# Feed-forward gate and up as seven half products per pair of blocks

## The chip, the cores and the metric

The kernel runs on one core of a Trainium2 chip. The metric is device time in microseconds of one launch. Before the change it is 1845.98 us, the median of three runs from 1844.38 to 1849.32. The engines named here are TensorE (PE, with its weight loads shown as PEld), VectorE (DVE), ScalarE (ACT), GpSimd (POOL) and the DMA queues, of which SP issues nearly all.

## The reference, cut to what matters

The kernel computes a whole two-part network for 512 rows of width 1024 in float32: a feed-forward layer, two attention branches that are merged, a second feed-forward layer, a chunkwise recurrent mixer and a gated linear recurrence, with norms and residuals between. Only the two feed-forward layers are touched:

```
def rms_norm(x, g):
    y = x * rsqrt(mean(x * x, axis=-1) + EPS)
    return y * g

def swiglu(x, w_gate, w_up, w_down):
    return (silu(x @ w_gate) * (x @ w_up)) @ w_down

h = h + 0.5 * swiglu(rms_norm(h, ffn1_norm), ffn1_w_gate, ffn1_w_up, ffn1_w_down)
...
h = h + 0.5 * swiglu(rms_norm(h, ffn2_norm), ffn2_w_gate, ffn2_w_up, ffn2_w_down)
```

The weights are 1024 by 2816 for gate and up and 2816 by 1024 for down.

## The kernel before, in words

Activations lie transposed: the 1024 features are 8 tiles of 128 partitions, each 512 columns (the rows of x) wide. These are `h[0..7]`. A float32 product is made as three fp32r products: every operand is split in a high part (a cast on ACT) and a low part (a subtraction on DVE), and `mm3` (L111) issues high by high, high by low and low by high into one PSUM bank.

`wload` (L92) brings 128 by 1024 weights (512 KB) by one DMA on SP into a `raw` buffer (3 of them), and splits them into `hi` and `lo` (5 buffers each; ACT L97, DVE L99). It is given a higher priority, so that the scheduler puts it ahead of other work. The order of the instructions on each engine is fixed when the program is built, by a scheduler that follows the order of the code and these priorities; an engine then runs its list in order.

`ffn` (L203) works in 22 blocks of 128 features of gate and up. `operand` (L132) makes the split operand from `h` times the norm's gain, without the row factor 1/rms; that factor is a column factor here, kept in `rb`, and is multiplied in when a bank is read out (L196, L216). So the first four groups (`pre`) can run before `stats` (L189) has made `rb`: sums of squares on PE (L170), a power on POOL (L178), a transpose on PE (L184), a copy on DVE (L186). A `group` (L143) is 8 blocks of the contraction by 3 matmuls of 512 columns, 24 matmuls. Each block takes one group for gate and one for up; then come tanh on ACT (L198), two products on DVE (L200, L217) and the split (L121, L123). After 8, 8 and 6 blocks the eight output tiles of down get their share (`wload(dn...)`, a group, and L223 adds it to `h`).

Pools that matter: `ap` has 40 buffers of 128 by 512 for activations, `xp` 18 more (`chain`), `pp` and `qp` 4 PSUM banks each (`bank`, `cbank`), `vp` 5 (`v`).

## Time and profile before

| what | before |
|---|---|
| median of three runs | 1845.98 us |
| the profiled execution, its own time | 1849.27 us |
| its span, first to last instruction | 1847.2 us |
| PE busy | 1822.0 us, 99% |
| DVE busy | 1083.3 us, 59% |
| ACT busy | 709.8 us, 38% |
| POOL busy | 23.9 us, 1% |
| mean granted TensorE clock | 0.996 |
| DMA moved | 169.53 MB, 92 GB/s |

The page counts matmuls as busy from issue to the modelled end, and they overlap; so PE's 99% says only that PE had nearly always something to do. How fast the work goes is read from the distance between the starts of neighbouring matmuls. The first feed-forward layer takes about 371 us of the span, the second about 364 us.

### The profile page before, as it was taken

The numbers are of one execution on the slowest core, as the hardware profiler recorded it, in microseconds if no ns is written. First come the engines' busy times: TensorE is split into PE (matmuls) and PEld (weight loads), VectorE is DVE, ScalarE is ACT, GpSimd is POOL, SyncE is SP. The second block draws the span as 40 slices with busy tenths as digits, with TensorE's granted clock in tenths as the row PEclk, the third lists the DMA queues.
The fourth block names the chain that finished last, engine by engine and source line by source line (L and its number), as shares of the span: only waits on it lengthen the run. The fifth ranks groups of instructions, "written<-read, shape, count | busy, mean of one in ns | idle before, by whom it ended". The sixth has DMA issues, their size and how long they took to land.

```text
span 1847.2 us, 21163 instructions
## 1 busy us (share of the span) xinstructions
PE 1822.0 (99%) x8320; PEld 1478.5 (80%) x8320; DVE 1083.3 (59%) x1728; ACT 709.8 (38%) x1050; POOL 23.9 (1%) x53
## 2 busy tenths in 40 slices
PE   8999999999999999999999999999999999999998
PEld 6888888877776688788888888788887888888886
DVE  5544535644646465543543566867467466788785
ACT  4322312424344533222222253533434344446762
POOL 0000000000000000000000000000000000000000
PEclk9999999999999999999999999999999999999999
DMA  5323232333322123232333232222232232232222
GB/s 185 103 92 102 92 103 83 100 101 102 112 69 69 46 91 103 80 103 92 99 95 103 71 122 81 80 80 92 69 102 86 74 103 69 90 97 90 89 69 80
DMA packets 50018, 169.53 MB, mean 92 GB/s; under 512 B 5760, under 2 KB 5888, under 8 KB 49920
## 3 DMA queue, kind: packets, MB, share of 16 engines
q1 hardware_dynamic: 48048, 164.91, 27.5%
q10 hardware_dynamic: 1872, 3.29, 0.5%
q8 instruction: 65, 1.06, 0.2%
q14 instruction: 33, 0.27, 0.0%
HBM read 164.77 MB, written 2.10 MB: 90 GB/s over the span
## 4 chain that ended last, share of the span: by engine, by line
PE 83%; issue 13%; DVE 2%; ACT 1%; POOL 1%; DMA 0%; SPq 0%; POOLq 0%; ACTq 0%; DVEq 0%
PE bank L112 25%; PE bank L114 25%; PE bank L113 25%; PE cbank L679 1%; PE cbank L447 1%; PE cbank L112 1%; PE cbank L113 1%; PE cbank L114 1%; PE cbank L415 1%; POOL small L178 1%; PE cbank L702 1%; PE cbank L703 1%; PE cbank L704 1%; PE cbank L384 0%; ACT hi L97 0%
## 5 line engine op out<-in xcount | busy, mean ns | idle before, releaser
L112 PE MATMUL bank<-act,hi 128*128 128x512 f32 x1944 | 761.2, 393 | 6.6 <-ACT act L138 6.5
L113 PE MATMUL bank<-act,hi 128*128 128x512 f32 x1944 | 761.1, 392 | 1.1 <-DVE act L123 0.5
L114 PE MATMUL bank<-act,lo 128*128 128x512 f32 x1944 | 760.1, 391 | 0.0
L97 ACT CAST hi<-raw 128x1024 fp32r<-128x1024 f32 (+2 forms) x315 | 323.2, 1027 | 829.5 <-PE bank L113 546.5
L99 DVE TENSOR_TENSOR lo<-raw,hi 128x1024 fp32r<-128x1024 f32 (+2 forms) x315 | 375.2, 1192 | 137.9 <-ACT hi L97 137.4
L112 PEld LDWEIGHTS bank<-act,hi 128*128 128x128 f32 x1944 | 366.3, 189 | 87.6 <-ACT act L138 6.5
L113 PEld LDWEIGHTS bank<-act,hi 128*128 128x128 f32 x1944 | 366.4, 188 | 81.7 <-DVE act L123 3.7
L114 PEld LDWEIGHTS bank<-act,lo 128*128 128x128 f32 x1944 | 366.6, 189 | 77.2 <-issue 1.9
L196 DVE TENSOR_TENSOR act<-bank,rb 128x512 f32<-128x512 f32 x70 | 48.3, 690 | 117.8 <-PE bank L114 117.7
L223 DVE SCALAR_TENSOR_TENSOR h<-bank,h 128x512 f32<-128x512 f32 x48 | 33.2, 692 | 112.2 <-PE bank L114 111.7
L216 DVE TENSOR_TENSOR act<-bank,rb 128x512 f32<-128x512 f32 x42 | 29.0, 691 | 101.1 <-PE bank L114 101.1
L112 PE MATMUL bank<-hi,act 128*128 128x512 f32 x224 | 87.8, 392 | 0.0
L114 PE MATMUL bank<-hi,act 128*128 128x512 f32 x224 | 87.3, 391 | 0.0
L113 PE MATMUL bank<-lo,act 128*128 128x512 f32 x224 | 87.2, 389 | 0.0
L121 ACT CAST act<-act 128x512 fp32r<-128x512 f32 x96 | 59.6, 621 | 69.2 <-DVE act L217 28.7
L123 DVE TENSOR_TENSOR act<-act 128x512 fp32r<-128x512 f32 x96 | 65.9, 686 | 12.9 <-ACT act L121 12.4
L802 DVE SCALAR_TENSOR_TENSOR act<-act,vec 128x511 f32<-128x511 f32 (+2 forms) x84 | 62.7, 746 | 1.7
L112 PE MATMUL bank<-chain,hi 128*128 128x512 f32 x160 | 62.7, 393 | 0.0
L114 PE MATMUL bank<-chain,lo 128*128 128x512 f32 x160 | 62.5, 391 | 0.0
L113 PE MATMUL bank<-chain,hi 128*128 128x512 f32 x160 | 62.3, 389 | 0.0
L198 ACT ACTIVATE act<-act 128x512 f32<-128x512 f32 x72 | 45.3, 629 | 30.8 <-DVE act L196 30.5
L200 DVE SCALAR_TENSOR_TENSOR act<-act 128x512 f32<-128x512 f32 x72 | 49.3, 685 | 8.7 <-ACT act L198 8.7
(231 smaller groups left out, 1577.8 us busy)
## 6 DMA issues: line engine op xcount, KB each, us to landing
raw<-in_gu_dram SPq DMA_DIRECT2D x88, 512.0 KB, 3.2
raw<-in_mh_dram SPq DMA_DIRECT2D x64, 512.0 KB, 3.2
raw<-in_win_dram SPq DMA_DIRECT2D x34, 512.0 KB, 3.2
raw<-in_dn_dram SPq DMA_DIRECT2D x32, 512.0 KB, 3.5
raw<-in_mo_dram SPq DMA_DIRECT2D x16, 512.0 KB, 3.2
raw<-in_dn_dram SPq DMA_DIRECT2D x16, 384.0 KB, 3.1
raw<-in_rxr_dram SPq DMA_DIRECT2D x12, 512.0 KB, 3.2
raw<-in_rg_dram SPq DMA_DIRECT2D x12, 512.0 KB, 3.3
```

The source lines that it names most:

```text
L97: S.copy(hi[:, :cols], raw[:, :cols])
L99: V.tensor_tensor(lo[:, :cols], raw[:, :cols], f(hi[:, :cols]), op=ALU.subtract)
L112: PE.matmul(ps, st[0], mv[0], start=start, stop=False)
L113: PE.matmul(ps, st[0], mv[1], start=False, stop=False)
L114: PE.matmul(ps, st[1], mv[0], start=False, stop=stop)
L121: S.copy(hi, x)
L123: V.tensor_tensor(lo, x, f(hi), op=ALU.subtract)
L196: V.tensor_tensor(g, ps, rb, op=ALU.mult)
L198: S.activation(th, g, AF.Tanh, scale=0.5)
L200: V.scalar_tensor_tensor(s, th, 1.0, g, op0=ALU.add, op1=ALU.mult)
L223: V.scalar_tensor_tensor(x[o], ps, 0.25, x[o], op0=ALU.mult, op1=ALU.add)
L802: V.scalar_tensor_tensor(c[:, s:], t[:, : T - s], vc(w, j * nt + i), c[:, s:], op0=ALU.mult, op1=ALU.add)
```

## The change

In both feed-forward layers the first four blocks stay as they were (`plain`). The other 18 are each done as a 2 by 2 product of halves: gate and up are the two rows of the weight side, the lower and upper half of the contraction (4 tiles of 128 each) its columns; the activations are cut in 256 left and 256 right columns. Strassen's scheme (in Winograd's form) makes this product with seven half products instead of eight, from four sums of weight halves (`s1` to `s4`) and four sums of activation halves (`t1` to `t4`). Each half product is 4 by 3 matmuls of 256 columns, so a block takes 84 matmuls of 256 columns in place of 48 of 512.

The activations are normalised first now (`xhalves`, with `rb`), and cut, summed and split once per layer. The weight sums are made per block: one by a DMA that adds onto what lies in SBUF (`G.dma_start` with `accum_op`, issued from POOL), the others by two additions on DVE (`sums`). Seven products go into three PSUM banks and come out through DVE additions. Down is done in chunks of 4 blocks: two output tiles beside each block (`between`), and the last six blocks at the end. `ap` has 34 buffers in place of 40, `raw` 4 in place of 3, and a new pool `gp` two buffers of 128 by 1024 (`four`), which other stages use too.

```diff
--- before.py
+++ after.py
@@ -46,9 +46,10 @@
-    ap = ctx.enter_context(tc.tile_pool(name="ap", bufs=40))
+    ap = ctx.enter_context(tc.tile_pool(name="ap", bufs=34))
     wp = ctx.enter_context(tc.tile_pool(name="wp", bufs=5))
     sp = ctx.enter_context(tc.tile_pool(name="sp", bufs=32))
+    gp = ctx.enter_context(tc.tile_pool(name="gp", bufs=2))
     hp = ctx.enter_context(tc.tile_pool(name="hp", bufs=KD))
     rp = ctx.enter_context(tc.tile_pool(name="rp", bufs=2))
     xp = ctx.enter_context(tc.tile_pool(name="xp", bufs=18))
@@ -91,7 +92,7 @@
     def wload(src, cols=WU):
         with tc.high_priority(offset=BOOST):
-            raw = wp.tile([P, WU], F32, tag="raw", name="raw", bufs=3)
+            raw = wp.tile([P, WU], F32, tag="raw", name="raw", bufs=4)
             nc.sync.dma_start(raw[:, :cols], src)
             hi = wp.tile([P, WU], F32R, tag="hi", name="hi")
             S.copy(hi[:, :cols], raw[:, :cols])
@@ -200,27 +201,207 @@
         V.scalar_tensor_tensor(s, th, 1.0, g, op0=ALU.add, op1=ALU.mult)
         return s
+    def raw_load(parts, adds):
+        raw = wp.tile([P, WU], F32, tag="raw", name="raw", bufs=4)
+        c = 0
+        for src in parts:
+            n = src.shape[-1]
+            nc.sync.dma_start(raw[:, c : c + n], src)
+            c += n
+        if adds is not None:
+            G.dma_start(raw.rearrange("p (r c) -> p r c", r=2), adds.unsqueeze(1).to_broadcast([P, 2, T]),
+                        accum_op=ALU.add)
+        return raw
+    def wsplit(raw):
+        hi = wp.tile([P, WU], F32R, tag="hi", name="hi")
+        S.copy(hi, raw)
+        lo = wp.tile([P, WU], F32R, tag="lo", name="lo")
+        V.tensor_tensor(lo, raw, f(hi), op=ALU.subtract)
+        return hi, lo
+    class Pair:
+        def __init__(self, top, low):
+            self.top, self.low, self.w = top, low, {}
+        def load(self):
+            top, low = self.top, self.low
+            with tc.high_priority(offset=BOOST):
+                self.r2 = raw_load([low[:, T:], top[:, :T]], low[:, :T])
+                self.r1 = raw_load([top], None)
+        def halves(self, raw, one, two):
+            hl = wsplit(raw)
+            self.w[one], self.w[two] = cut(hl, slice(0, T)), cut(hl, slice(T, WU))
+        def first(self):
+            with tc.high_priority(offset=BOOST):
+                self.halves(self.r1, "a11", "a12")
+                self.halves(self.r2, "s1", "s3")
+        def sums(self):
+            r1, r2 = self.r1, self.r2
+            with tc.high_priority(offset=BOOST):
+                V.tensor_tensor(r2[:, :T], r2[:, :T], r1[:, :T], op=ALU.add)
+                V.tensor_tensor(r2[:, T:], r2[:, :T], r1[:, T:], op=ALU.add)
+                self.halves(r2, "s2", "s4")
+        def last(self):
+            with tc.high_priority(offset=BOOST):
+                t = vp.tile([P, T + 32], F32, tag="v", name="v")
+                nc.sync.dma_start(t[:, :T], self.low[:, T:])
+                hi = vp.tile([P, T + 32], F32R, tag="v", name="v")
+                S.copy(hi[:, :T], t[:, :T])
+                lo = vp.tile([P, T + 32], F32R, tag="v", name="v")
+                V.tensor_tensor(lo[:, :T], t[:, :T], f(hi[:, :T]), op=ALU.subtract)
+            self.w["a22"] = cut((hi, lo), slice(0, T))
+    HT = T // 2
+    L, R = slice(0, HT), slice(HT, T)
+    def xhalves(x, gain, rb):
+        b = {n: [] for n in ("b11", "b21", "b22", "t1", "t2", "t3", "t4")}
+        def step(k):
+            xn = []
+            for i in (k, k + 4):
+                t = act_tile()
+                V.scalar_tensor_tensor(t, x[i], gain[:, i : i + 1], rb, op0=ALU.mult, op1=ALU.mult)
+                xn.append(t)
+            one, two = xn
+            b1 = act_tile(F32R)
+            S.copy(b1[:, L], one[:, L])
+            V.tensor_tensor(b1[:, R], one[:, L], f(b1[:, L]), op=ALU.subtract)
+            b["b11"].append((b1[:, L], b1[:, R]))
+            b2 = split(two)
+            b["b21"].append(cut(b2, L))
+            b["b22"].append(cut(b2, R))
+            t12, t34 = ctile(), ctile()
+            V.tensor_tensor(t12[:, L], one[:, L], one[:, R], op=ALU.subtract)
+            V.scalar_tensor_tensor(t12[:, R], t12[:, L], -1.0, two[:, R], op0=ALU.mult, op1=ALU.subtract)
+            V.tensor_tensor(t34[:, L], two[:, R], one[:, R], op=ALU.subtract)
+            V.scalar_tensor_tensor(t34[:, R], t12[:, R], -1.0, two[:, L], op0=ALU.mult, op1=ALU.subtract)
+            for t, n in ((t12, ("t1", "t2")), (t34, ("t3", "t4"))):
+                pr = split(t, ctile)
+                b[n[0]].append(cut(pr, L))
+                b[n[1]].append(cut(pr, R))
+        return b, step
+    def product(ps, w, xk):
+        for k in range(4):
+            mm3(ps, cut(w, slice(k * P, k * P + P)), xk[k], k == 0, k == 3)
+    def quarters(t):
+        return t.rearrange("p (r c) -> p r c", c=HT)
+    def twice(t):
+        return t.unsqueeze(1).to_broadcast([P, 2, HT])
+    def pair_products(pair, b, nxt, between):
+        w = pair.w
+        if nxt:
+            nxt.load()
+        m = bank()
+        product(m[:, L], w["a11"], b["b11"])
+        p1 = ctile()
+        with tc.high_priority(offset=EVAC):
+            S.copy(p1[:, L], m[:, L])
+        c1, c2 = cbank(), cbank()
+        product(c1[:, L], w["a12"], b["b21"])
+        if nxt:
+            nxt.first()
+        between(0)
+        product(c2[:, L], w["s1"], b["t1"])
+        product(c2[:, R], w["s3"], b["t3"])
+        product(c1[:, R], w["s2"], b["t2"])
+        t = gp.tile([P, 2 * T], F32, tag="four", name="four")
+        v = act_tile()
+        with tc.high_priority(offset=EVAC):
+            V.tensor_tensor(quarters(t)[:, 0:4:3], quarters(c1), twice(p1[:, L]), op=ALU.add)
+            V.tensor_tensor(quarters(v), quarters(c2), twice(t[:, 3 * HT :]), op=ALU.add)
+            V.scalar_tensor_tensor(t[:, 3 * HT :], c2[:, R], 1.0, v[:, L], op0=ALU.mult, op1=ALU.add)
+        between(1)
+        c3 = bank()
+        product(c3[:, L], w["s4"], b["b22"])
+        if nxt:
+            nxt.sums()
+        product(c3[:, R], w["a22"], b["t4"])
+        if nxt:
+            nxt.last()
+        with tc.high_priority(offset=EVAC):
+            V.tensor_tensor(t[:, HT : 3 * HT], c3, v, op=ALU.add)
+        g, u = t[:, :T], t[:, T:]
+        th = act_tile()
+        S.activation(th, g, AF.Tanh, scale=0.5)
+        V.scalar_tensor_tensor(g, th, 1.0, g, op0=ALU.add, op1=ALU.mult)
+        V.scalar_tensor_tensor(u, u, -1.0, g, op0=ALU.mult, op1=ALU.mult)
+        return split(u)
     def ffn(x, gain, gu, dn, pre=None):
         xs = operand(x, gain)
         pre = pre or [wload(gu[0])]
         pre = [group(pre[n] if n < len(pre) else wload(gu[n]), xs, (bank if n < 2 else cbank)()) for n in range(4)]
         _, rb = stats(x)
-        for k0 in range(0, KF, 8):
-            k1 = min(KF, k0 + 8)
-            pr = []
-            for j in range(k0, k1):
-                pg, pu = pre[2 * j : 2 * j + 2] if j < 2 else [group(wload(gu[2 * j + i]), xs) for i in range(2)]
-                s = silu2(pg, rb)
-                u = act_tile()
-                with tc.high_priority(offset=EVAC):
-                    V.tensor_tensor(u, pu, rb, op=ALU.mult)
-                V.tensor_tensor(u, u, s, op=ALU.mult)
-                pr.append(split(u))
-            for o in range(KD):
-                w = wload(dn[o][:, k0 * P : k1 * P], (k1 - k0) * P)
-                ps = group(w, pr)
-                with tc.high_priority(offset=EVAC):
-                    V.scalar_tensor_tensor(x[o], ps, 0.25, x[o], op0=ALU.mult, op1=ALU.add)
+        def plain(j):
+            pg, pu = pre[2 * j : 2 * j + 2] if j < 2 else [group(wload(gu[2 * j + i]), xs) for i in range(2)]
+            s = silu2(pg, rb)
+            u = act_tile()
+            with tc.high_priority(offset=EVAC):
+                V.tensor_tensor(u, pu, rb, op=ALU.mult)
+            V.tensor_tensor(u, u, s, op=ALU.mult)
+            return split(u)
+        def down(o, w, base, us):
+            ps = group(w, us, base=base)
+            with tc.high_priority(offset=EVAC):
+                V.scalar_tensor_tensor(x[o], ps, 0.25, x[o], op0=ALU.mult, op1=ALU.add)
+        def down_two(o, k0):
+            c = slice(k0 * P, k0 * P + T)
+            with tc.high_priority(offset=BOOST):
+                raw = raw_load([dn[o][:, c], dn[o + 1][:, c]], None)
+                return wsplit(raw)
+        b, step = xhalves(x, gain, rb)
+        pr = [plain(0), plain(1)]
+        for k in range(4):
+            step(k)
+        pr += [plain(2), plain(3)]
+        def down_job(j):
+            if j >= 20:
+                return lambda i: None
+            o, got, us = 2 * (j % 4), [], old
+            def step(i):
+                if i < 0:
+                    got.append(down_two(o, 4 * (j // 4 - 1)))
+                else:
+                    down(o + i, got[0], 4 * i, us)
+            return step
+        cur = Pair(gu[8], gu[9])
+        cur.load()
+        cur.first()
+        cur.sums()
+        cur.last()
+        old, new = pr, []
+        for j in range(4, KF):
+            nxt = Pair(gu[2 * j + 2], gu[2 * j + 3]) if j + 1 < KF else None
+            job = down_job(j)
+            job(-1)
+            new.append(pair_products(cur, b, nxt, job))
+            cur = nxt
+            if j % 4 == 3 and j < 19:
+                old, new = new, []
+        for o in range(KD):
+            dw = wload(dn[o][:, 16 * P :], 6 * P)
+            down(o, dw, 0, new)
     ffn(h, vc("g1", 0, 8), a["gu1"], a["dn1"], first)
@@ -262,8 +443,9 @@
         rope_t = {}
         def rope_tables():
+            both = gp.tile([P, 2 * T], F32, tag="four", name="four")
             for i in range(2):
-                t = act_tile()
+                t = both[:, i * T : (i + 1) * T]
                 S.dma_start(t, a["rope"][i])
                 rope_t[i] = t
@@ -299,9 +481,16 @@
             S.copy(vb, pv)
             bv.append(vb)
+        room = []
         def gate(i):
             ps = group(wload(win[i]), xs)
-            g = act_tile()
+            if i < 20:
+                if not room:
+                    room.append(gp.tile([P, 2 * T], F32, tag="four", name="four"))
+                g = room[0][:, (i - 18) * T : (i - 17) * T]
+            else:
+                g = act_tile()
             with tc.high_priority(offset=EVAC):
                 V.tensor_tensor(g, ps, rb, op=ALU.mult)
             S.activation(g, g, AF.Tanh, scale=0.5)
@@ -636,11 +825,12 @@
             for i in range(2):
                 w = wload(a["mh"][hd][12 + i])
                 w3 = tuple(z.rearrange("p (k m) -> p k m", k=4) for z in w)
+                both = gp.tile([P, 2 * T], F32, tag="four", name="four")
                 for m in range(2):
                     ps = bank()
                     for k in range(4):
                         mm3(ps, tuple(z[:, k, m * P : (m + 1) * P] for z in w3), xcs[k], k == 0, k == 3)
-                    t = act_tile()
+                    t = both[:, m * T : (m + 1) * T]
                     with tc.high_priority(offset=EVAC):
                         S.activation(t, ps, AF.Copy, scale=(1.0 / 32, 0.5)[i])
                     qk.append(t)```

The order on the engines changes in three places that matter below. First DVE, in the first feed-forward layer, from the copy of `rb` on. Before:

```order
L186 COPY rb<-cbank 128x512
L196 TENSOR_TENSOR act<-bank,rb 128x512
L200 SCALAR_TENSOR_TENSOR act<-act 128x512
L216 TENSOR_TENSOR act<-bank,rb 128x512
L217 TENSOR_TENSOR act<-act 128x512
L99 TENSOR_TENSOR lo<-raw,hi 128x1024
L123 TENSOR_TENSOR act<-act 128x512
L196 TENSOR_TENSOR act<-cbank,rb 128x512
```

And of the program after, the same place further on, where the second `plain` block ends and the first of the four steps of `xhalves` begins (line numbers are those of the changed kernel: L124 is the low part of a split, L271 the normalisation, L276 the low part of `b11`, L282 to L285 the sums `t1` to `t4`):

```order
L355 TENSOR_TENSOR act<-act 128x512
L220 TENSOR_TENSOR lo<-raw,hi 128x1024
L124 TENSOR_TENSOR act<-act 128x512
L271 SCALAR_TENSOR_TENSOR act<-h,vec,rb 128x512 x2
L276 TENSOR_TENSOR act<-act 128x256
L282 TENSOR_TENSOR chain<-act 128x256
L284 TENSOR_TENSOR chain<-act 128x256
L124 TENSOR_TENSOR act<-act 128x512
L283 SCALAR_TENSOR_TENSOR chain<-chain,act 128x256
L271 SCALAR_TENSOR_TENSOR act<-h,vec,rb 128x512
L285 SCALAR_TENSOR_TENSOR chain<-chain,act 128x256
L124 TENSOR_TENSOR chain<-chain 128x512
```

Where DVE went from block to block, it now has the four steps between block 1 and the reading out of block 2, whose first row (L197 from a `bank`) stands only near the end of the fourth step.

Second DVE again, in the middle of a layer. One block before (L196 to L123, with the splits of two weight tiles):

```order
L196 TENSOR_TENSOR act<-bank,rb 128x512
L99 TENSOR_TENSOR lo<-raw,hi 128x1024
L200 SCALAR_TENSOR_TENSOR act<-act 128x512
L216 TENSOR_TENSOR act<-bank,rb 128x512
L217 TENSOR_TENSOR act<-act 128x512
L99 TENSOR_TENSOR lo<-raw,hi 128x1024
L123 TENSOR_TENSOR act<-act 128x512
```

One block after, from the weight sums on (L247, L248 the sums, L220 the low part of a weight tile, L323 to L335 the reading out of the seven products, L258 the low part of `a22`, L361 the adding of down to `h`; L339, L340 and L124 stand behind L258):

```order
L247 TENSOR_TENSOR raw<-raw 128x512
L361 SCALAR_TENSOR_TENSOR h<-bank,h 128x512
L248 TENSOR_TENSOR raw<-raw 128x512
L220 TENSOR_TENSOR lo<-raw,hi 128x1024
L323 TENSOR_TENSOR four<-cbank,chain 128x2x256
L324 TENSOR_TENSOR act<-cbank,four 128x512
L325 SCALAR_TENSOR_TENSOR four<-cbank,act 128x256
L361 SCALAR_TENSOR_TENSOR h<-bank,h 128x512
L220 TENSOR_TENSOR lo<-raw,hi 128x1024 x2
L335 TENSOR_TENSOR four<-bank,act 128x512
L258 TENSOR_TENSOR v<-v 128x512
```

The splits of the next block's weights stand between the readings of this block's products, so each waits for the other in DVE's fixed order.

Third PE, at the start of the first layer, between the sums of squares and the transposes for `rb` (here with buffer numbers; `bank_343` before and `bank_446` after are the fifth group, the gate of block 2). Before:

```order
L114 MATMUL cbank_248<-act_151,lo_246 128x512
L170 MATMUL cbank_296<-ones_95,chain_293 128x1
L170 MATMUL cbank_296<-ones_95,chain_293 128x1 x3
L112 MATMUL bank_343<-act_123,hi_339 128x512
L113 MATMUL bank_343<-act_124,hi_339 128x512
L184 MATMUL cbank_304<-ident_90,small_301 128x128
```

After:

```order
L171 MATMUL cbank_299<-ones_98,chain_296 128x1 x3
L113 MATMUL bank_446<-act_126,hi_442 128x512
L114 MATMUL bank_446<-act_127,hi_442 128x512
L115 MATMUL bank_446<-act_126,lo_444 128x512
L113 MATMUL bank_446<-act_130,hi_442 128x512
L114 MATMUL bank_446<-act_131,hi_442 128x512
L115 MATMUL bank_446<-act_130,lo_444 128x512
L113 MATMUL bank_446<-act_134,hi_442 128x512
L114 MATMUL bank_446<-act_135,hi_442 128x512
L185 MATMUL cbank_307<-ident_93,small_304 128x128
```

Eight matmuls of the fifth group stand ahead of the transposes in place of two. On POOL two of the adding DMAs stand ahead of the power for `rb`.

## Rows read from the trace of the kernel before

**Rows 1.** The page, busy time, share and instructions by engine.
```profile
PE 1822.0 (99%) x8320; PEld 1478.5 (80%) x8320; DVE 1083.3 (59%) x1728; ACT 709.8 (38%) x1050; POOL 23.9 (1%) x53
```
**Rows 2.** Waits of PE: engine, line, for whom; total us, times, longest.
```profile
PE bank L112 <- ACT act L138: 6.5, 1, 6.5
PE cbank L184 <- POOL small L178: 4.2, 3, 1.8
```
**Rows 3.** Timeline of PE, 56 neighbouring matmuls of 512 columns: start, duration, instruction.
```profile
99.77 0.39 PE L112 MATMUL bank<-act,hi 128*128 128x512 f32 x1
...
112.23 0.39 PE L113 MATMUL bank<-act,hi 128*128 128x512 f32 x1
```
**Rows 4.** Timeline of PE in the mixer, 60 neighbouring matmuls of 256 columns.
```profile
1197.67 0.28 PE L702 MATMUL cbank<-v,act 128*128 128x256 f32 x1
...
1204.82 0.40 PE L112 MATMUL bank<-act,hi 128*128 128x512 f32 x1
```
**Rows 5.** Timeline of PEld at the same place.
```profile
1197.79 0.19 PEld L704 LDWEIGHTS cbank<-v,act 128*128 128x128 f32 x1
```
**Rows 6.** Windows by stage: length, busy us (instructions) by engine, PEclk, DMA share, GB/s.
```profile
0.00:371.00 371.00, 362.05 (x1577) 297.45 (x1578) 191.34 (x235) 119.12 (x145) 2.62 (x8) 1.00 0.33 107
```
**Rows 7.** Groups by form, DVE, first layer: shapes xcount | busy, mean ns.
```profile
L99 DVE TENSOR_TENSOR lo<-raw,hi 128x1024 fp32r<-128x1024 f32 x63 | 77.0, 1223 | 16.5 <-ACT hi L97 16.5
L217 DVE TENSOR_TENSOR act<-act 128x512 f32<-128x512 f32 x22 | 15.2, 691 | 0.6
```
**Rows 8.** Groups by form, DVE, the whole span.
```profile
L583 DVE SCALAR_TENSOR_TENSOR h<-h,vec,rb 128x512 f32<-128x512 f32 x8 | 5.8, 742 | 0.0
L707 DVE SCALAR_TENSOR_TENSOR chain<-chain,cbank 128x256 f32<-128x256 f32 x16 | 6.7, 416 | 9.1 <-PE cbank L704 9.1
```
**Rows 9.** Groups by form, ACT, first layer.
```profile
L97 ACT CAST hi<-raw 128x1024 fp32r<-128x1024 f32 x63 | 66.3, 1052 | 204.1 <-PE bank L113 144.3 <-issue 46.8 <-PE cbank L113 6.8
L198 ACT ACTIVATE act<-act 128x512 f32<-128x512 f32 x22 | 13.8, 628 | 10.4 <-DVE act L196 10.3
L121 ACT CAST act<-act 128x512 fp32r<-128x512 f32 x22 | 13.7, 621 | 14.3 <-DVE act L217 14.3
```
**Rows 10.** Timeline of PE around the transposes for `rb`, first layer.
```profile
33.81 0.49 PE L112 MATMUL bank<-act,hi 128*128 128x512 f32 x1
34.13 0.40 PE L113 MATMUL bank<-act,hi 128*128 128x512 f32 x1
36.23 0.65 PE L184 MATMUL cbank<-ident,small 128*128 128x128 f32 x4 [1.70 <-POOL small L178]
```
**Rows 11.** Timeline of POOL there.
```profile
34.30 1.87 POOL L178 TENSOR_TENSOR small<-small,mhalf 128x4 f32<-128x4 f32 x1 [32.92 <-DVE small L177]
```
**Rows 12.** Timeline of DVE from the copy of `rb` on.
```profile
36.91 0.69 DVE L186 COPY rb<-cbank 128x512 f32<-128x512 f32 x1 [1.62 <-PE cbank L184]
37.64 0.69 DVE L196 TENSOR_TENSOR act<-bank,rb 128x512 f32<-128x512 f32 x1
39.03 0.69 DVE L200 SCALAR_TENSOR_TENSOR act<-act 128x512 f32<-128x512 f32 x1 [0.69 <-ACT act L198]
39.64 0.68 DVE L216 TENSOR_TENSOR act<-bank,rb 128x512 f32<-128x512 f32 x1
40.35 0.69 DVE L217 TENSOR_TENSOR act<-act 128x512 f32<-128x512 f32 x1
...
59.85 0.69 DVE L216 TENSOR_TENSOR act<-bank,rb 128x512 f32<-128x512 f32 x1 [0.71 <-PE bank L114]
```
**Rows 13.** Windows behind the transposes, first and second layer (columns as rows 6).
```profile
36.20:40.20 4.00, 3.97 (x13) 3.21 (x14) 2.56 (x4) 0.63 (x1) 0.00 (x0) 0.61 0.39 131
753.40:757.50 4.10, 4.02 (x13) 3.30 (x14) 2.51 (x4) 0.63 (x1) 0.02 (x1) 0.58 0.38 132
```
**Rows 14.** DMA issues: out<-in, queue, op xcount, KB each, median us to landing.
```profile
raw<-in_gu_dram SPq DMA_DIRECT2D x88, 512.0 KB, 3.2
h<-in_xT_dram SPq DMA_DIRECT2D x8, 256.0 KB, 5.3
```

## Prediction

> **What bounds the kernel now.** I read the page's busy times first, then who waited for whom, then the timeline of PE. PE is busy 99% of the span, DVE 59%, ACT 38% [rows 1], and PE's two largest waits come to 6.5 and 4.2 us in the whole span [rows 2]. So the kernel goes at PE's pace, which stands in the distance of starts: 55 steps between matmuls of 512 columns take 12.46 us, 0.2266 each [rows 3]. A change pays if it takes time from that stream without making PE wait for DVE, which has room: 191 of 371 us in the first feed-forward layer [rows 6].
>
> **The PE work.** A block of gate and up is 48 matmuls of 512 columns, 48 x 0.2266 = 10.88 us. It becomes 84 of 256. The mixer's fp32r matmuls are of that kind: 60 of them from 1197.67 to 1204.82, 0.1192 each, every one with its own weight load of 0.19 us beside it [rows 4, 5]. 84 x 0.1192 = 10.01 us, so 0.87 us a block, 15.6 us for 18 blocks, 31.3 us for both layers. Strassen saves an eighth of the columns, but the fixed part of a matmul (two of 256 cost 0.2384, one of 512 costs 0.2266) takes back some of it. Down keeps its matmuls.
>
> The Trainium skill (TensorE: Matmul & The Clock Gate, "Back-to-back issue gap") gives columns/2.4 + 2.5 ns, which makes 109 and 216 ns; by it both layers would save 36 x (10.36 - 9.17) = 43 us. The rows are 10 ns above it at either width, and I keep to them.
>
> **DVE in the middle of a layer.** One block with its two down shares has on DVE 4 low parts of 1024 columns, 11 operations of 512 and one of 256: 4 x 1.22 + 11 x 0.69 + 0.42 = 12.9 us [rows 7, 8]. PE takes 10.01 + 24 x 0.2266 = 15.45 us for it. ACT has 4 casts of 1.05, one tanh, two casts and a copy: 6.5 us [rows 9]. So PE still sets the pace if the fixed order allows it. I count from a block's first product. The latest weights are those of down: their hi buffer comes free with the previous block's product with `s4` at -1.42; cast 1.05, low part 1.14 (1.22 less the overlap seen in rows 12), ready at 0.8; PE wants them after two products, at 2.86. That is 2 us to spare. Then follow the next block's `a11`/`a12` split, the reading of `c3` (from 2.1), `a22`, the two products behind tanh, the split of `s1`/`s3` and of the result (to 6.7), and sums and split for `s2`/`s4` by 11; the products that DVE then reads are done at 9.9, so it is up to 2 us late there and has made it good at 12.6. I cost a steady block at no wait. What is lost if that cover goes is rival 3.
>
> Three times in a layer a new chunk of down begins, which needs the result of the block just finished. Its high part is there at 5.5, PE comes to it at 4.9, and to its low part 0.2 us too early: 0.85 us, 2.6 us a layer. The bounds are 0 (PE fills in other products) and 2 us each (the `a22` cast in front on ACT is late). At the end of a layer the same chain lasts 4 us from the last product, and the five older blocks' 15 matmuls (3.4 us) and a second output tile lie beside it: nothing, as before.
>
> **The start of a layer.** Here PE will wait. In the first layer the copy of `rb` begins at 36.91 and blocks 0 and 1 follow [rows 12]. Operations of 512 columns there start 0.61 us apart, 0.71 if one needs the other, and a tanh between costs 0.70. After: twelve of 512, two splits of 1024 and two casts waited for take DVE from 37.64 to 48.8 (0.45 of it because the split of `s1`/`s3` needs a hi buffer that the fifth group holds until about 40.4, 16 matmuls after the transposes). Up to the low half of the last `b21`/`b22`, 34 more: 8 normalisations at 0.66 (0.742 [rows 8] less overlap), 16 of 256 columns at 0.36 (0.416 less overlap, some dependent), 10 splits at 0.61: 17.1 us, to 65.9. On POOL the power for `rb` now stands behind two adding DMAs, the second of which waits for loads into the buffer of the last plain weights. Those are split when the third group gives up its hi buffer (some 27 matmuls before 33.81, at 27.6; cast and low part to 29.9), and the loads land 3.2 us after issue [rows 14], at about 33.5; the power began at 34.30 [rows 11]. Issuing it costs POOL an unknown time: 0 to 1.9 us (the power's own length is the nearest row of POOL); I take 0.5, near nothing, since most of it lies before 34.3. So 66.4.
>
> PE meanwhile: 96 matmuls of groups five to eight. Before they go from 33.81 to 59.85 [rows 10, 12], 26.0 us where 96 x 0.2266 = 21.8 do, because PE stands still from 34.5 to 36.2 and then runs 4 us at a granted clock of 0.61, between its two levels of 1.2 and 2.4 GHz [rows 10, 13]. After, eight matmuls lie in that gap in place of two, 1.8 us of the 2.1; I take the clock to hold, 21.8 + 0.65 for the transposes + 0.6 of gap + 0.5 = 23.5, to 57.3. That is a gain of 2.5 (0 if the clock falls all the same). Then 20 products of 256 can run ahead (2.4 us) until the activations are whole: 66.4 - 57.3 - 2.4 = 6.7 us of waiting, with a slow clock behind it as after the gap of before, 4 us at 0.61, 1.6 us. Sum 8.3 - 2.5 = 5.8 us a layer. Bounds: 0 in all, and 15, if casts on ACT hold up each step as tanh does.
>
> The DMA that adds is not in the trace. It moves 512 KB; the nearest rows are 3.2 us for 512 KB and 5.3 for 256 KB in the crowd of the start [rows 14]. Its buffer is loaded a whole block ahead, and between the landing of what it adds to (about 4.5 in block n-2) and the cast (3.9 in block n-1) lie 14.8 us. Bounds 3 to 15 us, all hidden; I take 5.
>
> The Trainium skill (SBUF, "Who interferes with whom") says that DVE operations in a two-port mode keep POOL from writing the descriptors of its DMAs, while two-input ones like these do not. Nothing in this trace tests that, as POOL issues no DMA.
>
> The other stages keep their order but for short stretches; 34 + 4 buffers for 40 and a fourth `raw` I put at 0, within 3 us either way.
>
> **Sum.** A layer: -15.6 + 2.6 + 5.8 = -7.2; both -14.4. From the profiled execution's 1849.27 us (span 1847.2, 2.1 around it) that is 1834.9; that execution is 3.3 above the median, so 1831.6, say 1832 against 1845.98.
>
> **Rivals.**
> 1. Nothing waits: the preparation of the activations is covered and chunks follow smoothly. Then 2 x (15.6 + 2.5) = 36 us: 1810. For it: DVE's room. Against: DVE's rows behind `rb` are back to back for 28 us while PE has 21 us of work. Chance 0.14.
> 2. A matmul of 256 costs half of one of 512: 84 x 0.1133 = 9.52, 18 us more saved: 1814. Rows 4 speak against it. Chance 0.03. (By the page above it would be 1820.)
> 3. The steady block waits: weights late at PE in every block, because the adding DMA takes over 15 us or DVE's order, 84% full, runs into the 2 us to spare. From 0.4 us a block (14.4/36) on it eats the gain; at 1 us a block it is 36 us: 1868, slower. For it: each weight tile now passes DMA, DMA, DVE sum, ACT, DVE in a fixed order. Against: the spare time above. Chance 0.18.
> 4. The start waits 13 us a layer in place of 5.8: 1846, no change. For it: DVE waits for ACT at almost every step, and 0.70 each [rows 12] on 20 casts is 14 us. Against: most casts have another DVE operation beside them. Chance 0.20.
>
> **How the numbers follow.** The forecast (1822 to 1841 by itself) has 0.45. Within 0.3% of 1846, 1840.4 to 1851.5, is what cannot be told from no change. Faster: 0.42 of the forecast, 0.17 of rivals 1 and 2, 0.05 of 4: 0.64. Same: 0.03, 0.11 of 4, 0.02 of 3: 0.16. Slower: 0.16 of 3, 0.04 of 4: 0.20. The range 1812 to 1858 leaves out most of rival 1 and the upper half of rival 3.
>
> **What would show it.** The distance of 256-column matmuls in gate and up near 0.119 us; steady blocks of about 15.5 us; in PE's waits two stretches of 6 to 9 us at the start of the layers, on the DVE and ACT lines of `xhalves`, and a granted clock below 1 behind them; none on the weights inside a layer. Waits of PE on `hi` or `lo`, 18 times a layer, would be rival 3 and prove me wrong; a first product within 3 us of the last plain group would be rival 1.

## The result, and the profile after

The changed kernel takes 1880.19 us (median of four runs, 1878.55 to 1881.83) against 1847.02 for before on the same chip: ratio 1.018, 95% interval 1.0162 to 1.0198. That is 33 us slower, where 14 us faster was forecast, and outside the range of 1812 to 1858.

The page's first part after the change; compare [rows 1]. PE's busy time fell by only 5 us, and 60 us of the span are now without PE work where 25 were:

```profile
PE 1816.8 (97%) x9616; PEld 1528.2 (81%) x9616; DVE 1287.1 (69%) x2056; ACT 795.4 (42%) x1190; POOL 64.8 (3%) x89
```

The two feed-forward layers did get shorter. The table of windows shows this best, cut at each stage's last addition to `h`: first feed-forward, attention, second feed-forward, mLSTM (the chunkwise recurrent mixer), last mixer with the output. Columns as in [rows 6]; by this cut the first layer before ends at 376.3 us, not at the 371 of that row. Before:

```profile
0.00:376.30 376.30, 367.35 (x1601) 301.81 (x1602) 196.10 (x240) 122.73 (x149) 2.62 (x8) 1.00 0.33 108
376.30:729.30 353.00, 348.62 (x1665) 262.36 (x1664) 187.93 (x404) 141.59 (x288) 3.02 (x5) 1.00 0.26 85
729.30:1093.50 364.20, 362.45 (x1598) 299.64 (x1598) 178.62 (x221) 105.16 (x129) 1.93 (x1) 1.00 0.30 96
1093.50:1598.50 505.00, 503.54 (x2376) 416.08 (x2375) 336.93 (x592) 209.17 (x317) 14.32 (x37) 1.00 0.26 85
1598.50:1847.20 248.70, 240.07 (x1086) 198.61 (x1084) 183.76 (x273) 131.10 (x171) 2.03 (x2) 0.99 0.26 85
```

After:

```profile
0.00:371.10 371.10, 356.59 (x2249) 321.81 (x2250) 296.83 (x404) 164.79 (x219) 23.69 (x26) 0.99 0.55 151
371.10:726.30 355.20, 350.97 (x1666) 263.84 (x1665) 188.98 (x406) 143.21 (x290) 2.98 (x4) 0.99 0.27 85
726.30:1083.20 356.90, 352.21 (x2245) 320.21 (x2244) 278.42 (x382) 146.13 (x197) 23.09 (x20) 0.99 0.50 135
1083.20:1625.30 542.10, 516.21 (x2376) 424.04 (x2375) 339.25 (x592) 210.79 (x317) 13.01 (x37) 0.97 0.24 79
1625.30:1876.80 251.50, 240.79 (x1086) 198.31 (x1085) 183.64 (x273) 130.46 (x171) 2.03 (x2) 0.99 0.25 82
```

The differences are -5.2, +2.2, -7.3, +37.1 and +2.8 us, in sum +29.6, which is the difference of the two profiled spans (the medians lie 33 apart). All of the loss, and more, lies in a stage whose matmuls the change does not touch: mLSTM has 2376 of them in both kernels. PE's waits there, after the change:

```profile
PE bank L113 <- ACT act L122: 24.3, 5, 6.7
PE cbank L185 <- DVE small L722: 0.9, 1, 0.9
PE cbank L764 <- DVE chain L757: 0.5, 1, 0.5
```

Before, PE's waits in this stage came to 1.2 us:

```profile
PE cbank L184 <- DVE small L533: 0.9, 1, 0.9
PE cbank L575 <- DVE chain L568: 0.3, 1, 0.3
```

L122 is the cast of `split`. Here it stands behind the convolution (`conv`, L989 and L992) of the mLSTM's `x_conv`, whose result `qk_proj` takes as its operand. Three of the five waits lie in the first head. Timeline of PE there:

```profile
1170.08 2.07 PE L113 MATMUL bank<-act,hi 128*128 128x512 f32 x4 [6.71 <-ACT act L122]
...
1179.82 0.80 PE L113 MATMUL bank<-act,hi 128*128 128x512 f32 x1 [4.87 <-ACT act L122]
...
1189.94 0.80 PE L113 MATMUL bank<-act,hi 128*128 128x512 f32 x1 [4.86 <-ACT act L122]
```

And of DVE, the first operation of the second, third and fourth convolution:

```profile
1162.94 0.54 DVE L989 TENSOR_SCALAR act<-act,vec 128x512 f32<-128x512 f32 x1
...
1174.77 0.55 DVE L989 TENSOR_SCALAR act<-act,vec 128x512 f32<-128x512 f32 x1 [1.88 <-PE bank L114]
...
1184.88 0.55 DVE L989 TENSOR_SCALAR act<-act,vec 128x512 f32<-128x512 f32 x1 [4.39 <-PE bank L114]
```

Read together they are a ring. DVE waits for PE: the convolution gets its `act` buffer only when the matmuls of `qk_proj` have read the split before it. PE then waits for the convolution's own split. Each turn costs 10 us, and PE works for half of them. In the kernel before, the four convolutions of the first head began at 1147.9, 1155.7, 1164.7 and 1172.0, 7 to 9 us apart and early enough that PE never waited for them; after the change the first begins at 1137.6 and the second only at 1162.9.

The rest of the 37 us goes with the clock. PE's waits rose by 24.5 us, its busy time by 12.7 with the same matmuls. The granted clock there (the figure behind POOL's):

```profile
1170.00:1177.00 7.00, 4.88 (x12) 3.39 (x12) 5.02 (x10) 2.18 (x6) 1.26 (x8) 0.71 0.27 76
1177.00:1184.00 7.00, 4.18 (x9) 3.10 (x10) 2.05 (x3) 1.97 (x3) 0.00 (x0) 0.54 0.00 0
1184.00:1191.00 7.00, 2.14 (x6) 1.14 (x6) 4.18 (x6) 1.60 (x3) 0.00 (x0) 0.74 0.00 0
1191.00:1198.00 7.00, 7.00 (x20) 4.70 (x19) 2.50 (x3) 4.62 (x7) 0.00 (x0) 0.74 0.21 74
```

A mean of 0.54 is a stretch nearly all at 1.2 GHz. PE stood still for 4.9 to 6.7 us ahead of it, and the matmuls behind the wait pay again. The Trainium skill (TensorE: Matmul & The Clock Gate, "What's actually happening") says that idleness halves PE's clock and that sustained work gives it back; these rows agree.

### The profile page after: what moved, and what is told of

Read it like the earlier page. It is cut to its first block, busy times and chain, and to the rows that moved or that the text cites. A ratio compares the mean times of both kernels' runs of the same rounds, so it can differ in the third digit from the quotient of the medians.

```text
span 1876.8 us, 24687 instructions
## 1 busy us (share of the span) xinstructions
PE 1816.8 (97%) x9616; PEld 1528.2 (81%) x9616; DVE 1287.1 (69%) x2056; ACT 795.4 (42%) x1190; POOL 64.8 (3%) x89
## 4 chain that ended last, share of the span: by engine, by line
PE 78%; issue 13%; DVE 6%; ACT 2%; DMA 1%; POOL 1%; SPq 0%; POOLq 0%; ACTq 0%; DVEq 0%
PE bank L113 20%; PE bank L114 20%; PE bank L115 19%; PE cbank L114 4%; PE cbank L113 4%; PE cbank L115 4%; PE cbank L869 1%; PE cbank L636 1%; PE cbank L604 1%; DVE act L992 1%; DMA raw<-in_gu_dram 1%; PE cbank L893 1%; ACT hi L98 1%; DVE act L271 1%; PE cbank L894 1%
## 5 line engine op out<-in xcount | busy, mean ns | idle before, releaser
L113 PE MATMUL bank<-act,hi 128*128 128x512 f32 (+1 forms) x1656 | 625.2, 379 | 32.3 <-ACT act L122 24.8
L114 PE MATMUL bank<-act,hi 128*128 128x512 f32 (+1 forms) x1656 | 623.9, 377 | 1.2 <-DVE act L140 0.7
L115 PE MATMUL bank<-act,lo 128*128 128x512 f32 (+1 forms) x1656 | 620.2, 375 | 1.3 <-DVE lo L100 1.3
L98 ACT CAST hi<-raw 128x1024 fp32r<-128x1024 f32 (+2 forms) x211 | 213.3, 1014 | 427.5 <-PE bank L114 241.3
L113 PEld LDWEIGHTS bank<-act,hi 128*128 128x128 f32 x1656 | 316.1, 191 | 93.4 <-ACT act L122 28.2
L114 PEld LDWEIGHTS bank<-act,hi 128*128 128x128 f32 x1656 | 316.2, 191 | 60.0 <-DVE act L124 4.0
L115 PEld LDWEIGHTS bank<-act,lo 128*128 128x128 f32 x1656 | 316.0, 191 | 57.4 <-issue 1.9
L100 DVE TENSOR_TENSOR lo<-raw,hi 128x1024 fp32r<-128x1024 f32 (+2 forms) x211 | 248.1, 1177 | 152.7 <-ACT hi L98 151.8
L218 ACT CAST hi<-raw 128x1024 fp32r<-128x1024 f32 x140 | 146.4, 1050 | 246.8 <-PE cbank L114 108.7
L220 DVE TENSOR_TENSOR lo<-raw,hi 128x1024 fp32r<-128x1024 f32 x140 | 170.6, 1224 | 78.4 <-ACT hi L218 78.4
L113 PE MATMUL cbank<-chain,hi 128*128 128x256 f32 x432 | 123.3, 286 | 2.5 <-ACT chain L122 2.3
L114 PE MATMUL cbank<-chain,hi 128*128 128x256 f32 x432 | 122.9, 285 | 2.2 <-DVE chain L124 2.2
L115 PE MATMUL cbank<-chain,lo 128*128 128x256 f32 x432 | 122.7, 284 | 0.0
L114 PE MATMUL cbank<-act,hi 128*128 128x256 f32 (+1 forms) x264 | 88.2, 334 | 2.2 <-DVE act L124 2.2
L113 PE MATMUL cbank<-act,hi 128*128 128x256 f32 (+1 forms) x264 | 88.5, 335 | 1.5 <-ACT act L122 1.3
L114 PE MATMUL bank<-lo,act 128*128 128x512 f32 x224 | 88.3, 394 | 0.0
L113 PE MATMUL bank<-hi,act 128*128 128x512 f32 x224 | 88.2, 394 | 0.0
L113 PEld LDWEIGHTS cbank<-chain,hi 128*128 128x128 f32 x432 | 83.5, 193 | 5.2 <-ACT chain L122 3.2
L115 PE MATMUL bank<-hi,act 128*128 128x512 f32 x224 | 87.7, 392 | 0.0
L115 PE MATMUL cbank<-act,lo 128*128 128x256 f32 (+1 forms) x264 | 87.7, 332 | 0.0
L114 PEld LDWEIGHTS cbank<-chain,hi 128*128 128x128 f32 x432 | 83.1, 193 | 4.6 <-DVE chain L124 3.1
L115 PEld LDWEIGHTS cbank<-chain,lo 128*128 128x128 f32 x432 | 83.3, 193 | 0.1
## 6 DMA issues: line engine op xcount, KB each, us to landing
raw<-in_mh_dram SPq DMA_DIRECT2D x64, 512.0 KB, 3.5
raw<-in_gu_dram SPq DMA_DIRECT2D x52, 512.0 KB, 3.6
raw<-in_gu_dram SPq DMA_DIRECT2D x72, 256.0 KB, 2.9
raw<-in_gu_dram POOLq DMA_DIRECT2D x36, 512.0 KB, 6.1
raw<-in_win_dram SPq DMA_DIRECT2D x34, 512.0 KB, 3.5
raw<-in_dn_dram SPq DMA_DIRECT2D x64, 256.0 KB, 2.9
v<-in_gu_dram SPq DMA_DIRECT2D x36, 256.0 KB, 2.8
raw<-in_mo_dram SPq DMA_DIRECT2D x16, 512.0 KB, 3.5
```

What stands on the lines that cost most here:

```text
L98: S.copy(hi[:, :cols], raw[:, :cols])
L100: V.tensor_tensor(lo[:, :cols], raw[:, :cols], f(hi[:, :cols]), op=ALU.subtract)
L113: PE.matmul(ps, st[0], mv[0], start=start, stop=False)
L114: PE.matmul(ps, st[0], mv[1], start=False, stop=False)
L115: PE.matmul(ps, st[1], mv[0], start=False, stop=stop)
L218: S.copy(hi, raw)
```

## The experiments

I put two explanations against each other. Theory B: the pool. With 34 `act` buffers in place of 40 the mLSTM stage is short of them. Counted in the code, when `x_conv` of the first head ends it holds 16 (`xs`), 8 (`xm`), 4 (`z2`), 4 convolutions and their 8 splits, 40. In the next two heads `v_proj` has run first, so 4 low parts of `v` stand in place of the 8: 36. In the last head `o_proj`, the last to read `xs`, stands ahead of `qk_proj` and gives those 16 back. So 34 are 6 short once and 2 short twice. Rival C: the new feed-forward code (order, weight transfers) disturbs what follows.

**Only the pools.** The lines of the diff on `ap`, `gp`, `raw` and on `four` in the other stages, with `ffn` as before.

> The kernel before with only the buffers of the change (34 act buffers and the two wide ones that hold rope, gates, q and k, in place of 40; four raw weight buffers in place of three); its feed-forward is the plain one. Theory B (buffers): the time was lost in the mLSTM stage, because its x_conv holds up to 40 act buffers in the first head and 36 in the next two, so with 34 the convolutions wait for the matmuls of qk_proj to give theirs back and TensorE waits for the convolutions. The mLSTM stage (last add of the second feed-forward to its own last add) then takes 538 to 546 us, as after the change (542.1), against 505.0 before, with five PE waits on the high cast of split of 24 us in all; the whole kernel 1880 to 1900 us, since the gain of the feed-forward is not in it. Rival C (the new feed-forward code itself, through the order that the scheduler builds or the weight transfers that it leaves behind, disturbs what follows): mLSTM 505 +-4 us, the kernel 1843 to 1852.

1889.6 us, ratio 1.0229 (1.0213 to 1.0246). The mLSTM stage, and PE's first wait in it:

```profile
1091.10:1632.20 541.10, 515.19 (x2376) 423.34 (x2376) 339.38 (x593) 210.77 (x316) 12.90 (x37) 0.97 0.23 79
```
```profile
PE bank L113 <- ACT act L122: 24.3, 5, 6.7
```

The same five waits without any of the new feed-forward code. Rival C falls. The plain layers themselves (375.1 and 362.5 us) did not suffer from 34 buffers.

**Two buffers more, one weight buffer fewer.**

```diff
-    ap = ctx.enter_context(tc.tile_pool(name="ap", bufs=34))
+    ap = ctx.enter_context(tc.tile_pool(name="ap", bufs=36))
-            raw = wp.tile([P, WU], F32, tag="raw", name="raw", bufs=4)
+            raw = wp.tile([P, WU], F32, tag="raw", name="raw", bufs=3)
```

> The changed kernel with 36 act buffers and three raw weight buffers in place of 34 and four, which is the same memory. Theory B: the second and third heads need 36 and fit, so their two stalls (3.9 us each and 3.4 us each for the slow clock behind them) go, and of the three of the first head one goes (about 5 us and 3 of slow clock): mLSTM about 520 us (514 to 526) in place of 542.1. The feed-forward may pay for the third raw buffer: 0 to 10 us a layer. Kernel 1856 to 1878. Rival C: mLSTM 538 to 546, the kernel 1876 or more. Rival C2 (the fourth raw buffer, by earlier weight transfers, is what disturbs the mLSTM stage): mLSTM back to 505 +-4.

1875.09 us, ratio 1.0153 (1.0137 to 1.0168). mLSTM 513.9 us, two waits left, both in the first head:

```profile
PE bank L113 <- ACT act L122: 6.0, 2, 5.8
```

```profile
1198.35 1.22 PE L113 MATMUL bank<-act,hi 128*128 128x512 f32 x2 [5.81 <-ACT act L122]
...
1204.39 1.19 PE L113 MATMUL bank<-act,hi 128*128 128x512 f32 x4 [0.23 <-ACT act L122]
```

The waits of the second and third head went, as the count says; of the first head's three, one went, as expected, but a second shrank to 0.2 us, so the stage came out just under the 514 to 526 expected. The feed-forward paid more than I allowed: 386.8 and 371.6 us, 15.7 and 14.7 more, with PE waits of 22.8 and 14.9 us, now on weights too. In the first layer from 100 us on, where there were none:

```profile
PE bank L115 <- DVE lo L220: 5.1, 3, 2.7
PE bank L113 <- ACT act L122: 3.8, 2, 2.9
PE bank L113 <- ACT hi L218: 1.0, 2, 0.5
```

This edit changes two pools at once; the new waits on `lo` and `hi` are waits on weights, which pass through `raw` and not through `ap`. So the fourth `raw` buffer is what the seven products need, and the memory for it was taken from a pool that a later stage needs.

**The mLSTM stage in an order that needs 34.**

```diff
         x_proj(0)
-        z_proj(0)
         gate_rows()
+        v_proj(0)
         x_conv(0)
...
         qk_proj(0)
+        z_proj(0)
...
-            (o_proj if hd else v_proj)(hd)
+            if hd:
+                o_proj(hd)
             numer(hd)
-            z_proj(hd + 1)
+            z_proj(hd + 1, 0, 2 if hd < 2 else 4)
...
             qk_proj(hd + 1)
+            if hd < 2:
+                z_proj(hd + 1, 2, 4)
```

> The changed kernel with the mLSTM stage written in an order that holds at most 34 act buffers: v_proj(0) ahead of x_conv(0) (it frees eight), z_proj(0) behind qk_proj(0), and of z_proj(1) and z_proj(2) two groups behind qk_proj. Buffers, pools and feed-forward as after the change. Theory B: the stalls go, mLSTM 505 to 511 us, the kernel 1840 to 1850 us, so at or just under the kernel before. Rival C: stalls stay, mLSTM 535 or more, the kernel 1873 or more.

1840.7 us (10 runs), ratio 0.9971 (0.9962 to 0.9981): 39.5 us faster than the changed kernel and faster than before. The mLSTM stage is back at its old length, with its old PE time, though the fourth `raw` buffer is kept, so rival C2 (the fourth `raw` buffer as the cause) falls as well:

```profile
1081.70:1586.90 505.20, 503.58 (x2376) 416.08 (x2375) 337.82 (x592) 209.89 (x316) 12.33 (x37) 1.00 0.25 85
```

**Two buffers held in the kernel before.**

```diff
+        held = [act_tile() for _ in range(2)]
+        with tc.high_priority(offset=1000):
+            for t in held:
+                G.memset(t[:, :1], 0.0)
         x_proj(0)
...
             qk_proj(hd + 1)
+        for t in held:
+            G.tensor_copy(t[:, :1], st[3]["qk"][0][:, :1])
         scores(3)
```

> The kernel before, in which two act buffers are held (one column written, nothing read from it) from the start of the mLSTM heads to qk_proj of the last: 38 in place of 40, nothing else changed. Theory B: only the first head, which needs 40, is short, by one convolution: one PE wait of 4 to 6 us and about 3.4 us more for the slow clock, mLSTM 510 to 515, the kernel 1852 to 1858. Rival C, or that the 40 leave room to spare: no wait, the kernel 1847 +-3.

1853.52 us, ratio 1.0041 (1.0027 to 1.0056). mLSTM 512.6 us, and PE's new wait:

```profile
PE bank L112 <- ACT act L121: 4.9, 1, 4.9
```

So the kernel before had at most one to spare. 38, 36 and 34 buffers cost the stage 7.6, 8.9 and 37.1 us (the last two with q and k in the new pool).

**The second adding DMA behind the power.** Built on the mended order of 1840.7 us, as are the next three.

```diff
-        def load(self):
+        def load(self, offset=BOOST):
-            with tc.high_priority(offset=BOOST):
+            with tc.high_priority(offset=offset):
...
-            new.append(pair_products(cur, b, nxt, job))
+            new.append(pair_products(cur, b, nxt, job, -300 if j == 4 else BOOST))
```

> The changed kernel with the mLSTM order of the run before (1840.7 us), and with the loads of the second pair of a layer at a lower priority, so that on POOL its adding DMA stands behind the power for rb and not ahead of it. Theory P: in the first layer POOL stood before that DMA for 7.9 us until its target was loaded, and so the copy of rb began at 39.8 us in place of 36.9; with the order turned it begins at about 37.4 and the layer is 2 us shorter (1 to 3), the second layer 0 to 0.5; kernel 1837 to 1840. Rival: the chain behind rb is not what the start of the layer waits for, or the second pair's weights now come late by as much: no change, 1839 to 1843.

1840.22 us, ratio 0.9962 (0.995 to 0.9974): no change from 1840.7. The copy of `rb` does begin at 37.5 us in place of 39.7, but the first layer takes 372.6 us in place of 371.3. PE's waits in it fell by 1.0 us only, and the granted clock from 60 to 100 us is 0.87 in place of 0.91. The traces show what held it in place of `rb`. In the kernel that this one is built on, DVE waits 0.42 us for the cast of the next weights; here 3.38 us, as the cast needs a `hi` buffer that matmuls on PE must give back first:

```profile
45.04 1.22 DVE L220 TENSOR_TENSOR lo<-raw,hi 128x1024 fp32r<-128x1024 f32 x1 [3.38 <-ACT hi L218]
```
```profile
43.95 1.05 ACT L218 CAST hi<-raw 128x1024 fp32r<-128x1024 f32 x1 [4.35 <-PE bank L114]
```

And those matmuls ran slower: from 36 to 42 us the granted clock was 1.00 in the kernel it is built on (first line) and 0.72 here.

```profile
36.00:42.00 6.00, 3.30 (x18) 2.58 (x17) 1.61 (x3) 0.63 (x1) 2.28 (x2) 1.00 0.54 89
```
```profile
36.00:42.00 6.00, 5.16 (x18) 4.18 (x19) 3.37 (x5) 0.63 (x1) 2.02 (x2) 0.72 0.42 62
```

So the first step of `xhalves` begins at 52.38 us in place of 51.55, although `rb` is there 2.1 us earlier.

**Two outputs of down ahead of the first products.**

```diff
             job(-1)
+            if j == 4:
+                job(0)
+                job(1)
+                job = lambda i: None
             new.append(pair_products(cur, b, nxt, job))
```

> The changed kernel with the mLSTM order of 1840.7 us, and with the first two outputs of the first down chunk (24 matmuls of 512 columns, 5.4 us) ahead of the first pair's products in place of between them. Theory S: TensorE's waits of 4.3 us on the transformed activations, and 3.4 us or less of slow clock behind them, are filled with these matmuls: 3 to 7 us a layer, kernel 1827 to 1835. Rival: they wait themselves, since they need the result of the last plain block about 3 us after its matmuls, or the weights of down come later than the pair's: under 1 us a layer, kernel 1838 to 1843.

1842.05 us, ratio 0.9965 (0.9952 to 0.9977); the rival holds. In the second layer the waiting products stand from 774 to 781 us, and down's matmuls come behind them, from 782.5: first in the code is not first on the engine. Whether their weights or the last plain block made them late was not told apart.

**Fewer `act` buffers in the last mixer.** The two temporaries of `silu2` (`g`, `th`) come from `mk`.

```diff
-            st[p]["z2"] = [silu2(group(wload(a["rg"][3 * p + j]), xs), rb) for j in range(3)]
+            st[p]["z2"] = [silu2(group(wload(a["rg"][3 * p + j]), xs), rb, ctile) for j in range(3)]
```

> The changed kernel with the mLSTM order of 1840.7 us, and with the two temporaries of each gate projection in the last mixer (RG-LRU) in the chain pool in place of the act pool. Theory B: the last stage too is short of act buffers, since it takes 251.8 us with 34 and 248.8 with 36; with fewer in use it falls to 248.5 to 250, kernel 1837 to 1839. Rival: other buffers than these are short there, or the chain pool gets short: 251 or more.

1839.61 us, ratio 0.9954 (0.9941 to 0.9967). The last stage takes 248.9 us, 2.9 less than in the kernel it is built on, as in the kernel before: theory B for this stage too.

**All three.**

> The three edits together. If all three theories hold their gains add: 2 + 8 + 3 = 13 us less than 1840.7, so 1824 to 1833; if only the first and the last hold, 1834 to 1838; if none, 1840 to 1843. The second edit may make the first worth less, since both act on the start of a layer.

1836.07 us (1835.78 to 1838.85), ratio 0.9941 (0.9929 to 0.9953), the fastest that leaves nothing out: 11.5 us under before, 44 under the change as it was made. That lies in the range for the first and the last theory, but the stages do not bear the first one out: against the kernel of 1840.7 us the first layer is 0.9 us longer, the second 0.6 shorter, the last mixer 2.7 shorter, and the attention stage, which no edit touches, 1.9 shorter.

**The plain feed-forward in that kernel.** `ffn` of before, all else kept.

> The fastest kernel so far (1836.1 us: changed feed-forward, mLSTM order and the gate temporaries of the last mixer mended), with the plain feed-forward of before put back and everything else kept, the pools of the change too. Theory F: the feed-forward change is worth by itself what the earlier run with the new pools alone leaves for it, 9.4 us (1889.6 - 1880.2), up to the 14.4 of the prediction: this kernel 1845 to 1851. Rival: the gain of 1836 over before comes from the mended order of the other stages and not from the feed-forward: 1835 to 1840.

1848.73 us (11 runs), ratio 1.0011 (1.0003 to 1.002). So the feed-forward is worth 12.7 us here (1848.73 - 1836.07), but that holds the two edits at its start. As it was made it is worth 9.1 (1848.73 - 1839.61), which agrees with the 9.4 that the run with the pools alone leaves for it (1889.6 - 1880.2): some 9 us of the 14.4 forecast. The mended order of the other stages gives nothing without it.

**No transforms.** This kernel leaves out the four sums of activation halves and their splits; the plain quarters stand in their place, so its output is not that of the reference.

```diff
-            t12, t34 = ctile(), ctile()
...
+            for n, m in (("t1", "b21"), ("t2", "b22"), ("t3", "b22"), ("t4", "b21")):
+                b[n].append(b[m][-1])
```

> The kernel of 1836.1 us, with the four transformed activation quarters of each pair of rows left out: the plain quarters stand in their place, so gate and up are not those of the reference. It keeps all products and their matmuls. Theory S: the wait at the start of a layer (4.3 us in small pieces on the splits of the transforms, and 6.8 us of slow clock behind it, about 3 us lost) goes, since DVE has 16 operations of 256 columns and 8 low parts less there: 5 to 8 us a layer, kernel 1820 to 1827. Rival: the start is held by rb and the plain blocks in front on DVE, and the transforms lie beside other work: under 2 us a layer, kernel 1832 to 1838.

1821.07 us, ratio 0.9865 (0.9849 to 0.988): 15.0 us less than 1836.07. In the traces the layers are 7.7 and 6.3 us shorter, and the clock stays up; first the kernel of 1836.07, then this one:

```profile
60.00:100.00 40.00, 35.67 (x215) 31.52 (x215) 37.84 (x62) 18.07 (x27) 2.41 (x2) 0.91 0.36 91
```

```profile
60.00:100.00 40.00, 39.39 (x268) 36.13 (x267) 34.24 (x48) 17.98 (x26) 2.76 (x3) 1.00 0.46 122
```

## Why the prediction was wrong, step by step

**The step that failed** is the sentence that stands last before the sum: "34 + 4 buffers for 40 and a fourth `raw` I put at 0, within 3 us either way." They cost 42.4 us with the pools alone (1889.6 - 1847.2). I had looked at what the new buffers serve and not at what the stages outside the diff hold at their fullest. The cost rested on no row, and the shortage could have been counted from the code. No rival had it, and no other term takes the time out of the range: with the mLSTM order mended the kernel takes 1840.7 us, with the last mixer mended too 1839.6, which is 6.5 and 8.0 us under before on the same chip, where 14.4 was forecast.

**PE work, -15.6 a layer.** Right in kind. In the changed kernel 24 steps between matmuls of 256 columns, 2.87 us, 0.1196 each where [rows 4] gave 0.1192:

```profile
151.67 0.28 PE L113 MATMUL cbank<-chain,hi 128*128 128x256 f32 x1
...
154.54 0.28 PE L113 MATMUL cbank<-chain,hi 128*128 128x256 f32 x1
```

That makes 84 x 0.1196 = 10.05 us a block and -15.0 a layer. Rival 2 falls. The formula of the Trainium skill (TensorE: Matmul & The Clock Gate, "Back-to-back issue gap") gives 109 ns; the trace stays 10 ns above it, so the rows were the better ground.

**The steady block, no wait.** Right. From 100 us to the end of the first layer PE shows no wait at all, with DVE busy for 81%, and four blocks of the second layer take 62.4 us (910.80 to 973.16), 15.6 each where 15.45 was worked out:

```profile
100.00:371.10 271.10, 271.10 (x1824) 251.07 (x1824) 218.82 (x282) 117.70 (x151) 16.84 (x14) 1.00 0.56 151
```

The adding DMA takes 6.1 us at the median where 5 was taken. Rival 3 falls for this kernel, but three `raw` buffers bring it: 15 us a layer.

**New chunks of down, +2.6.** Too high. In the second layer the three places show 0.2 us each beyond the usual distances, 0.6 in all.

**The start of a layer, 8.3 less 2.5.** The 8.3 was near: leaving out the transforms gives back 7.7 and 6.3. It is made up otherwise, of shorter waits and a longer slow clock (0.60 from 64 to 68 us and 0.55 from 68 to 72 in the first layer). PE's waits in the second layer:

```profile
PE cbank L114 <- DVE chain L124: 1.2, 2, 0.6
PE cbank L113 <- ACT chain L122: 1.2, 1, 1.2
PE cbank L114 <- DVE act L124: 1.1, 2, 0.8
PE cbank L113 <- ACT act L122: 0.8, 1, 0.8
PE cbank L185 <- POOL small L179: 0.4, 1, 0.4
```

4.3 us on the halves of the activations and their sums where 6.7 were forecast. The last line is the gain that eight matmuls ahead of the transposes bring: 0.4 against 1.8. In the first layer PE waited 2.6 us there against 1.7 before, by the term that I took at 0.5, POOL's power behind two adding DMAs. Timeline of POOL:

```profile
27.48 1.38 POOL L212 DMA_DIRECT2D raw<-in_gu_dram  x1 [26.10 <-DMA raw<-in_gu_dram]
36.78 1.21 POOL L212 DMA_DIRECT2D raw<-in_gu_dram  x1 [7.92 <-DMA raw<-in_gu_dram]
37.54 1.52 POOL L179 TENSOR_TENSOR small<-small,mhalf 128x4 f32<-128x4 f32 x1
```

The issue itself takes 1.2 us, but POOL stands before it for 7.9 us until the tile it adds to has landed, and the power begins 3.2 us later than in [rows 11]. I had the landing at 33.5; it came at 36.8. Yet this term does not set the length of the layer by itself: with the power ahead of the second DMA PE's wait was 1.7 again, but the clock fell behind it and DVE waited for a `hi` buffer, and the layer was no shorter (372.6 us).

**The sum.** -7.2 a layer was forecast; -5.2 came in the first and -7.3 in the second. Part of the match is luck. Against the plain layers in the same pools (375.1 and 362.5 us) it is -4.0 and -5.6 only. And in the second layer the terms differ from those forecast: -15.0, +0.6, and for the start of the second layer +5.5 (9.2 us of distances beyond the usual after, 3.7 before) make -8.9, and 1.6 us I did not place.

**The other stages.** Besides mLSTM, the last mixer lost 2.8 us to the same shortage (248.8 us with 36 buffers, 248.9 with its temporaries moved). The 2.2 us of the attention stage are not the change's: its waits did not grow, and over the kernels with the changed feed-forward it took 351.3 to 355.2 us, as the granted clock fell there (to 0.91 over 20 us) twice (355.1 and more), once (353.6 and 353.8) or not at all (351.3 and 351.9).

## What to carry to other kernels

A buffer taken from a shared pool is paid for in the stage that is fullest, not in the stage that is edited: count, for every stage, what lives at its fullest place, before a pool is made smaller. A shortage shows as a ring in the waits, where the bottleneck engine waits for an engine that waits for the bottleneck engine, and here the order of the code mended it, which returned 37 us. When a result contradicts a sum, cut the span by stage first: the terms of the sum can be right and the loss where no term was.

## What the hardware showed that was not expected

A wait cost more than itself: 24.3 us of waits in five places came with 12.7 us more of PE's busy time, and one wait of 4.9 us in the kernel with two buffers held made its stage 7.6 us longer. At the lower clock (from 1181.1 us after) matmuls of 512 columns stand 0.43 us apart, against 0.2266 at the upper.

A DMA that adds onto SBUF held up its engine's queue: POOL, not the DMA queue, waited 7.9 us for the tile to land, with the power of the norm behind it.
